# A macaron decoder layer: how the feed-forwards are multiplied, and how their sums reach the residual

## The chip, the core and the metric

The kernel runs on one core of a Trainium2 chip. Its engines are TensorE (matmuls; PE in the profile, its weight loads PEld), VectorE (DVE), ScalarE (ACT), GpSimd (POOL) and SyncE (SP, which here only issues DMAs). Each engine works through its own instruction queue in order, and semaphores make one wait for another. The metric is the device time of one execution in microseconds: the median of three runs is 2218.06 us (2217.84 to 2219.36).

## What is computed

One decoder layer over 256 tokens of width 2048, in float32: a feed-forward, a token mixer, a cross-attention, a second feed-forward and a final norm. The change touches the two feed-forwards:

```python
def rms_norm(x, g):
    xf = x.astype(jnp.float32)
    y = xf * lax.rsqrt(jnp.mean(xf * xf, axis=-1, keepdims=True) + NORM_EPS)
    return (y * g.astype(jnp.float32)).astype(x.dtype)

def swiglu(h, w_gate, w_up, w_down):
    return (jax.nn.silu(h @ w_gate) * (h @ w_up)) @ w_down

x = x + 0.5 * swiglu(rms_norm(x, ffn1_norm[l]), ffn1_w_gate[l], ffn1_w_up[l], ffn1_w_down[l])
...
x = x + 0.5 * swiglu(rms_norm(x, ffn2_norm[l]), ffn2_w_gate[l], ffn2_w_up[l], ffn2_w_down[l])
```

w_gate and w_up are 2048 x 5632, w_down is 5632 x 2048.

## The kernel before, in words

**A product in three matmuls.** Every float32 operand is split into two parts, `hi` (rounded, by ScalarE) and `lo` (what is left, by VectorE); a product is then hi*hi + hi*lo + lo*hi, three matmuls (`times`, L442 to L444). The stationary operand is 128 rows of x by 128 tokens, the moving one 128 rows by 512 columns of a weight. The sum of a product grows in a PSUM bank of 128 x 512; banks come from three rings, `acc` (3), `mm` (3) and `tr` (2, also used for transposes).

**Units, items, blocks.** A weight matrix is walked in column blocks of 512. A unit is two row groups of 128 x 512 (0.5 MB) of one block. An item is what the loop takes next (`next_item`, L401): one unit, or a pair of units of two matrices. A feed-forward has eleven column blocks j of gate and up, in groups of 4, 4 and 3, and behind each group the rows of w_down that belong to it, as two products: columns 0 and 512 together (first half), then 1024 and 1536 (second half).

**Seven products in place of eight.** From block 1 on, gate and up (and in w_down two column blocks) are multiplied together by `product_pair` (L502). For an ordinary pair q of rows it makes 2 token halves x 2 matrices x 2 row groups = 8 products, 24 matmuls. For the pairs listed in `SEVEN` (0, 2, 4) it makes seven products of sums and differences, 21 matmuls. These need sums of the weights (four VectorE steps, L394 to L397, split again by L373 and L374) and sums of x (`combinations`, L454, made once per feed-forward for x and once per group for the hidden values). `SEVEN_DOWN` does the same for w_down: (2, 4, 6) in the first half of a group of four, (2, 4) elsewhere (the second half of the last group of the second feed-forward is not paired). After the last of the seven-product pairs `middle` adds the banks p1, p5, p6, p7 into shared sums, and after the last pair `out` adds the other banks, p2, p4, p3, p5, as they end. In w_down each of these steps ends in x += 0.5 * bank (L603).

**Block 0** is not paired: first all eight units of gate (`product`, bank `acc`), then all eight of up (bank `mm`), while x_t, the transposed x, is still coming in by DMA in pieces (`chunks`) between the first weight loads. Features of x are made from x_t as it comes, and x itself is loaded later (`tokens`) for the mean square, whose root `norm.r` is needed only at the end of the block.

**What sets the order.** `next_item` issues the loads ahead on SyncE, in the order of the plan, and splits at most two units (one pair) ahead. There are three buffers of `hi` and of `lo`, one of each of the split weight sums (`thi`, `tlo`, a and b), and four of the 1 MB weight tiles; a load waits until its buffer is free. Between matmuls the loop ticks a set of generators (`Interleave`), which issue the transposes, the combinations of x and the loads of x a piece at a time. The program order is then rearranged once, ahead of the run, by a scheduler that goes by planned costs: it puts each engine's instructions in the order in which it expects their inputs, so that TensorE may take a later product ahead of one whose operand it expects late. On the chip these queues are fixed.

In the second feed-forward (`last`) the pairs with seven products are `SEVEN_2` = (0, 2, 3, 4); the weight sums of pair 3 are made earlier, in the mixer, and staged in DRAM at the items `STAGE_AT`.

## Time and profile before

| | |
|---|---|
| median of three runs | 2218.06 us (2217.84 to 2219.36) |
| the profiled execution | 2216.97 us |
| its span, first to last instruction | 2215.2 us |
| TensorE matmul busy | 2200.2 us (99%), 10520 matmuls |
| VectorE busy | 1829.0 us (83%) |
| ScalarE busy | 1250.0 us (56%) |
| DMA | 466.02 MB, mean 210 GB/s |

In the rows that follow, "out<-in" are the program's own names, then come the shapes, the count (x...), and, in a view by groups, the busy time and the mean duration of one, and behind a bar the idle time just before and what ended it. In a view in order of time a row begins with its start and its duration, and brackets at the end hold the idle time before it and its cause. In a view by stretch the busy time of each engine is followed by its count of instructions. L numbers are lines of the kernel before.

### The profile page before, as it was taken

How to read it: one execution, taken by the hardware profiler on the slowest of the kernel's cores; microseconds unless marked ns; L12 is line 12 of the kernel's file. 1: busy time of each engine (PE TensorE's matmuls, PEld its weight loads, DVE VectorE, ACT ScalarE, POOL GpSimd, SP SyncE). 2: the span in 40 equal slices, each digit the busy share in tenths (PEclk: the TensorE clock that was granted, in tenths of full speed). 3: DMA queues.
4: the chain of work that ended last, by engine and by line, in shares of the span. 5: the costliest groups of instructions: out<-in, count | busy, mean ns of one | idle time of the engine just before them, and what ended most of it. 6: DMA issues, size and time to landing. Idle time of an engine off the chain costs nothing.

```text
span 2215.2 us, 28140 instructions
## 1 busy us (share of the span) xinstructions
PE 2200.2 (99%) x10520; PEld 1817.0 (82%) x10520; DVE 1829.0 (83%) x2348; ACT 1250.0 (56%) x1621; POOL 107.0 (5%) x185
## 2 busy tenths in 40 slices
PE   9999999999999999999999999999999999999998
PEld 7888888888888877788888888888888888888886
DVE  7999988898989476977667666558999999999997
ACT  7555555555556477644544546556565565555654
POOL 0000000000000000000331130001000000000000
PEclk9999999999999999999999999999999999999999
DMA  8555555555556545676768687547665666665573
GB/s 306 199 207 198 194 200 201 198 199 194 200 194 204 178 130 165 197 237 210 223 224 287 209 273 270 183 164 280 220 221 190 212 227 211 214 208 208 200 244 135
DMA packets 231560, 466.02 MB, mean 210 GB/s; under 512 B 15520, under 2 KB 17920, under 8 KB 231424
## 3 DMA queue, kind: packets, MB, share of 16 engines
q1 hardware_dynamic: 222256, 438.08, 58.4%
q0 software_dynamic: 7648, 23.52, 3.5%
q10 hardware_dynamic: 1520, 2.63, 0.3%
q8 instruction: 82, 1.34, 0.3%
q14 instruction: 54, 0.44, 0.1%
HBM read 440.49 MB, written 23.59 MB: 209 GB/s over the span
## 4 chain that ended last, share of the span: by engine, by line
PE 94%; DVE 3%; DMA 1%; issue 1%; ACT 1%; SPq 0%; POOLq 0%; POOL 0%; DVEq 0%; ACTq 0%
PE acc L442 19%; PE acc L443 19%; PE acc L444 19%; PE mm L443 8%; PE mm L444 8%; PE mm L442 8%; PE tr L443 2%; PE tr L630 2%; PE tr L442 2%; PE tr L444 2%; PE mm L1425 1%; DVE lo L366 1%; DMA raw<-in_ffn_w_up_dram 1%; PE tr L1355 0%; ACT hi L365 0%
## 5 line engine op out<-in xcount | busy, mean ns | idle before, releaser
L365 ACT CAST hi<-raw 128x1024 fp32r<-128x1024 f32 (+1 forms) x768 | 755.1, 993 | 687.7 <-PE acc L444 485.9
L366 DVE TENSOR_TENSOR lo<-raw,hi 128x1024 fp32r<-128x1024 f32 (+1 forms) x768 | 878.8, 1147 | 291.8 <-ACT hi L365 289.3
L442 PE MATMUL acc<-hi,xhi 128*128 128x512 f32 (+1 forms) x1134 | 445.7, 394 | 2.0 <-DVE ga L1278 1.5
L443 PE MATMUL acc<-lo,xhi 128*128 128x512 f32 (+1 forms) x1134 | 439.9, 388 | 0.8 <-DVE lo L366 0.8
L444 PE MATMUL acc<-hi,xlo 128*128 128x512 f32 (+1 forms) x1134 | 439.7, 388 | 0.0
L442 PEld LDWEIGHTS acc<-hi,xhi 128*128 128x128 f32 x1134 | 213.2, 188 | 47.8 <-issue 3.1
L444 PEld LDWEIGHTS acc<-hi,xlo 128*128 128x128 f32 x1134 | 212.9, 188 | 43.5 <-issue 0.4
L443 PEld LDWEIGHTS acc<-lo,xhi 128*128 128x128 f32 x1134 | 213.4, 188 | 42.7 <-DVE lo L366 2.2
L373 ACT CAST thi<-raw 128x1024 fp32r<-128x1024 f32 x192 | 200.3, 1052 | 69.1 <-DVE raw L396 45.0
L374 DVE TENSOR_TENSOR tlo<-raw,thi 128x1024 fp32r<-128x1024 f32 x192 | 232.1, 1217 | 0.9 <-ACT thi L373 0.3
L442 PE MATMUL mm<-hi,xhi 128*128 128x512 f32 x402 | 156.6, 389 | 0.1
L443 PE MATMUL mm<-lo,xhi 128*128 128x512 f32 x402 | 156.5, 389 | 0.0
L444 PE MATMUL mm<-hi,xlo 128*128 128x512 f32 x402 | 156.4, 389 | 0.0
L444 PE MATMUL acc<-hi,hlo 128*128 128x512 f32 x372 | 145.4, 391 | 0.0
L443 PE MATMUL acc<-lo,hhi 128*128 128x512 f32 x372 | 145.3, 391 | 0.0
L442 PE MATMUL acc<-hi,hhi 128*128 128x512 f32 x372 | 145.0, 390 | 0.0
L442 PEld LDWEIGHTS mm<-hi,xhi 128*128 128x128 f32 x402 | 75.4, 188 | 16.2 <-ACT hi L365 0.5
L443 PEld LDWEIGHTS mm<-lo,xhi 128*128 128x128 f32 x402 | 75.5, 188 | 15.8
L444 PEld LDWEIGHTS mm<-hi,xlo 128*128 128x128 f32 x402 | 75.5, 188 | 15.7
L442 PEld LDWEIGHTS acc<-hi,hhi 128*128 128x128 f32 x372 | 69.9, 188 | 14.3
L443 PEld LDWEIGHTS acc<-lo,hhi 128*128 128x128 f32 x372 | 69.8, 188 | 14.3
L444 PEld LDWEIGHTS acc<-hi,hlo 128*128 128x128 f32 x372 | 69.9, 188 | 14.0
(443 smaller groups left out, 3526.6 us busy)
## 6 DMA issues: line engine op xcount, KB each, us to landing
raw<-in_ffn_w_down_dram SPq DMA_DIRECT2D x88, 1024.0 KB, 5.2
raw<-in_ffn_w_gate_dram SPq DMA_DIRECT2D x84, 1024.0 KB, 5.1
raw<-in_ffn_w_up_dram SPq DMA_DIRECT2D x78, 1024.0 KB, 6.0
raw<-in_w_in_dram SPq DMA_DIRECT2D x136, 512.0 KB, 3.8
...
```

Of the source, the lines that this page charges most:

```text
L365: at["hi"] = act.copy(hi[:, s], raw[:, s])
L366: at["lo"] = dve.tensor_tensor(lo[:, s], raw[:, s], f32(hi[:, s]), ALU.subtract)
L373: act.copy(hi[:], v[:])
L374: dve.tensor_tensor(lo[:], v[:], f32(hi[:]), ALU.subtract)
L442: pe.matmul(o, xh, hi, start=first, stop=False, **how)
L443: pe.matmul(o, xh, lo, start=False, stop=False, **how)
L444: pe.matmul(o, xl, hi, start=False, stop=last, **how)
L630: pe.transpose(b[:, o : o + P], tok[:, t, col : col + P], ident[:])
L1425: pe.matmul(vb[to, (o + k) * P : (o + k + 1) * P][:, r], lhs(k, e), v[:, k, r], start=v is u and k + e == 0, stop=True, **ek,)
```

## The change

- **Block 0 of the first feed-forward**: gate and up become one paired entry of eight items, multiplied by the new `plain_pair`: for every pair of row groups first gate (two `acc` banks), then up (two `mm` banks), 24 matmuls an item. The first loads on SyncE are put in that order: gate and up alternate, and the pieces of x_t follow their use. The first four units are split by halves. The loads of x and the squares are tied to other items (4 and 5 up to 7, of 8).
- **Seven more pairs with seven products** in the first feed-forward: blocks 3, 5, 7, 9, 10 use pairs (0, 2, 4, 6); blocks 4, 6, 8 use (2, 4, 6); blocks 1 and 2 keep (0, 2, 4). The second half of w_down uses (2, 4, 6) in the groups of four. Combinations of x are made for pair 6 too, from item 19 on. An early ordinary pair without a combination (pair 5, and pair 0 in blocks 4, 6, 8) adds its last product to a further bank, "q", as w_down did already, so `out` has one more addition.
- **w_down, both feed-forwards**: before the first matmul of a product pair, ScalarE writes twice x into the four banks p2, p4, p3 and q; the matmuls add to it, and what comes out is halved. `first` and `middle` then write into x itself. A pair has eight VectorE steps in place of twelve, and five ScalarE steps in place of one.
- Two constant tiles that nothing used ("shift", "pad") go; the staging is bound to items eight lower, since there are eight items fewer.

```diff
-                yield (wg, wu), 0, KD, (j * 512, j * 512), SEVEN_2 if last else SEVEN
+                seven = SEVEN_MORE if j in MORE else SEVEN_LATER if j in LATER_ON else SEVEN
+                seven = SEVEN_2 if last else seven
+                yield (wg, wu), 0, KD, (j * 512, j * 512), seven
...
+SEVEN_MORE, MORE = (0, 2, 4, 6), (3, 5, 7, 9, 10)
+SEVEN_LATER, LATER_ON = (2, 4, 6), (4, 6, 8)
 SEVEN_2, STAGED = (0, 2, 3, 4), (3,)
-STAGE_AT = [266 + 2 * n for n in range(10)]
+STAGE_AT = [258 + 2 * n for n in range(10)]
...
+            if j == 0 and not last:
+                yield (wg, wu), 0, KD, (0, 0), ()
...
-            yield (wd, wd), 4 * j0, 4 * nj, (1024, 1536), SEVEN_DOWN[1]
+            yield (wd, wd), 4 * j0, 4 * nj, (1024, 1536), SEVEN_DOWN[last or nj < 4]
...
-        for s in (slice(0, 1), slice(1, 2)) if u < AHEAD else (rows,):
+        for s in (slice(0, 1), slice(1, 2)) if u < 2 * AHEAD else (rows,):
...
+        for to, there in onto:
+            b[to] = rings[to]()
+            act.activation(b[to][:], there, AF.Copy, scale=2.0)
+            begun.add(to)
...
+    def plain_pair(sp, x: Act, norm, w):
+        pw, _, nk, _, seven = plan[at["product"]]
+        assert pw[0].tensor is w.tensor and not seven
+        at["product"] += 1
+        hb = sp.tile([P, 2, 512], F32, tag="hb", name="hb", bufs=2)
+        g2_, u2_ = [acc() for _ in range(2)], [mm() for _ in range(2)]
+        for k in range(0, nk, KU):
+            bg.until(lambda: all(k + i in x.done for i in range(KU)))
+            for wt, o in zip(next_item(), (g2_, u2_)):
+                for t in range(2):
+                    multiply(o[t][:], x, wt, k, t, nk)
+                    bg.tick()
+        bg.until(lambda: norm.r is not None)
+        for t in range(2):
+            act.activation(hb[:, t, :], g2_[t][:], AF.Silu, scale=norm.r[t])
+            dve.scalar_tensor_tensor(
+                hb[:, t, :], u2_[t][:], norm.r[t], hb[:, t, :], ALU.mult, ALU.mult
+            )
+        return hb
...
+                for z in (to, "q") if t and "q" in b else (to,):
+                    dve.tensor_tensor(v[:], b[z][:], v[:], ALU.add)
...
+    def down(h: Act, c, w, xs):
+        (x00, x01), (x10, x11) = xs
+        def half(x_, v, y):
+            dve.scalar_tensor_tensor(x_, v, 0.5, y, ALU.mult, ALU.add)
         def first(b):
-            act.copy(u3[:], b["p1"][:])
-            half(xs[0][0], b["p1"][:])
-            half(xs[1][1], b["q"][:])
+            act.activation(x00, b["p1"][:], AF.Copy, scale=0.5)
         def middle(b):
-            dve.tensor_tensor(u2[:], b["p6"][:], u3[:], ALU.add)
-            dve.tensor_tensor(u3[:], b["p7"][:], u2[:], ALU.add)
-            dve.tensor_tensor(u2[:], b["p5"][:], u2[:], ALU.add)
-            half(xs[1][0], u3[:])
-            half(xs[1][1], u3[:])
-            half(xs[0][1], u2[:])
+            half(x01, b["p6"][:], x00)
+            half(x10, b["p7"][:], x01)
+            half(x01, b["p5"][:], x01)
+            half(x11, b["q"][:], x10)
         def out(b, to):
-            half(xs[int(to in ("p4", "p5"))][int(to in ("p3", "p5"))], b[to][:])
-        product_pair(h, c, w, first, middle, out)
+            x_ = xs[int(to in ("p4", "p5"))][int(to in ("p3", "p5"))]
+            half(x_, b[to][:], x_)
+        product_pair(
+            h, c, w, first, middle, out, (("p2", x00), ("p4", x10), ("p3", x01), ("q", x11))
+        )
...
+            lambda q: (
+                at["item"] > begun + (18 if q > 4 and not last else 4)
+                and not (last and norm.r is None)
+            ),
+            less=(1,) if last else (1, 3),
...
+        load(2, [(slice(0, 2), nc.sync)])
         chunks(2, 2)
-        load_rest(0, 2, 1)
-        load_rest(0, 3, 1)
+        load_rest(0, 2)
+        load_rest(2, 2)
         chunks(4, 2)
-        load(2, [(slice(0, 2), nc.sync)])
+        load(4, [(slice(0, 2), nc.sync)])
+        load(6, [(slice(0, 2), nc.sync)])
         chunks(6, 2)
-        load_rest(2, 2)
+        load_rest(4, 2)
+        load_rest(6, 2)
         chunks(8, 4)
-        load(4)
         chunks(12, 4)
-        load(6)
         n1.begin(turned)
         def tokens(n):
-            while at["item"] < 7 + n:
+            while at["item"] < 4 + n // 2:
                 yield
             with tc.issue_after(at["hi"].ins):
                 act.dma_start(col(n), blk(W["x"], n))
-            while at["item"] < 10 + n:
+            while at["item"] < 5 + (n + 1) // 2:
...
```

61 lines of the change are left out of this document (26 added, 35 removed).

## Prediction

> **What bounds the kernel now.** I read the page first (busy shares, chain), then the busy time by stretch, then the waits of VectorE and ScalarE, then the order of time at the start and around a block of gate and up. The page:
>
> ```profile
> span 2215.2 us, 28140 instructions
> PE 2200.2 (99%) x10520; PEld 1817.0 (82%) x10520; DVE 1829.0 (83%) x2348; ACT 1250.0 (56%) x1621; POOL 107.0 (5%) x185
> PE 94%; DVE 3%; DMA 1%; issue 1%; ACT 1%; SPq 0%; POOLq 0%; POOL 0%; DVEq 0%; ACTq 0%
> raw<-in_ffn_w_gate_dram SPq DMA_DIRECT2D x84, 1024.0 KB, 5.1
> raw<-in_ffn_w_up_dram SPq DMA_DIRECT2D x78, 1024.0 KB, 6.0
> ```
>
> The chain is TensorE for 94%. The next view gives the first feed-forward as two stretches (busy time of each engine, then clock, DMA share, GB/s), two blocks inside it (j = 5 and 6), and five microseconds of the start:
>
> ```profile
> 4.92:52.08 47.16, 45.59 (x194) 36.02 (x193) 37.68 (x65) 35.09 (x60) 2.22 (x3) 1.00 0.94 343
> 52.08:710.10 658.02, 657.96 (x2949) 543.60 (x2949) 603.83 (x750) 367.24 (x417) 1.47 (x2) 1.00 0.57 198
> ...
> 306.20:348.60 42.40, 42.40 (x193) 35.20 (x192) 38.73 (x47) 24.49 (x28) 0.00 (x0) 1.00 0.58 199
> 348.60:390.90 42.30, 42.30 (x192) 35.14 (x191) 38.10 (x49) 23.34 (x26) 0.00 (x0) 1.00 0.57 199
> ...
> 20.00:25.00 5.00, 5.00 (x24) 4.10 (x23) 4.32 (x7) 2.95 (x5) 0.00 (x0) 1.00 1.05 386
> ```
>
> From 52.08 on TensorE is always busy, but VectorE is close behind: 603.8 of 658.0 us (92%), 54 us idle. The waits say what that idle time is:
>
> ```profile
> DVE lo L366 <- ACT hi L365: 39.0, 47, 1.8
> DVE raw L394 <- DMA raw<-in_ffn_w_up_dram: 4.8, 8, 0.9
> ...
> ACT hi L365 <- PE acc L444: 123.9, 94, 2.9
> ACT hi L365 <- PE mm L444: 72.7, 48, 2.1
> ```
>
> VectorE waits for ScalarE's `hi`, and ScalarE waits for TensorE to give back one of the three `hi` buffers. So VectorE idles because it has caught up, and those 39 us are its reserve.
>
> **Durations.** TensorE, in order of time (start, duration):
>
> ```profile
> 4.92 1.20 PE L442 MATMUL acc<-hi,xhi 128*128 128x512 f32 x2
> ...
> 7.49 0.50 PE L442 MATMUL acc<-hi,xhi 128*128 128x512 f32 x1 [0.52 <-ACT hi L669]
> ...
> 9.23 0.61 PE L442 MATMUL acc<-hi,xhi 128*128 128x512 f32 x2
> ...
> 44.18 0.39 PE L442 MATMUL mm<-hi,xhi 128*128 128x512 f32 x1
> ...
> 51.43 0.39 PE L444 MATMUL mm<-hi,xlo 128*128 128x512 f32 x1
> 52.08 0.73 PE L442 MATMUL tr<-thi,chi 128*128 128x512 f32 x2 [0.26 <-ACT thi L373]
> ```
>
> Between 44.18 and 51.43 lie 32 matmuls: 7.25 / 32 = 0.2266 us each, whatever their listed 0.39. VectorE overlaps in the same way; before and after block 6 begins at 348.6:
>
> ```profile
> 325.82 0.68 DVE L366 TENSOR_TENSOR lo<-raw,hi 128x512 fp32r<-128x512 f32 x1
> 327.92 1.23 DVE L366 TENSOR_TENSOR lo<-raw,hi 128x1024 fp32r<-128x1024 f32 x1 [1.42 <-ACT hi L365]
> ...
> 349.46 0.68 DVE L394 TENSOR_TENSOR raw<-raw,raw 128x512 f32<-128x512 f32 x1
> 350.06 0.74 DVE L593 SCALAR_TENSOR_TENSOR hb<-u,rs,hb 128x512 f32<-128x512 f32 x1
> 350.72 1.22 DVE L366 TENSOR_TENSOR lo<-raw,hi 128x1024 fp32r<-128x1024 f32 x1
> 351.86 0.68 DVE L395 TENSOR_TENSOR raw<-raw 128x512 f32<-128x512 f32 x1
> ...
> 354.80 1.22 DVE L374 TENSOR_TENSOR tlo<-raw,thi 128x1024 fp32r<-128x1024 f32 x1
> 355.94 1.81 DVE L366 TENSOR_TENSOR lo<-raw,hi 128x1024 fp32r<-128x1024 f32 x2
> ```
>
> Start to start: 0.60 for 128x512, 1.14 for 128x1024, 0.66 for the scaled one. An ordinary pair costs VectorE two `lo` = 2.3 us and TensorE 24 matmuls = 5.44 us. A pair with seven products costs VectorE four sums, three wide `lo` and a half one, 4 x 0.60 + 3 x 1.14 + 0.60 = 6.4 us, and TensorE 21 matmuls = 4.76 us.
>
> **The change, part by part.**
> Seven more pairs: five in blocks 3, 5, 7, 9, 10, two in the second halves of w_down. 7 x 3 = 21 matmuls leave TensorE: -4.76 us, on the path.
>
> VectorE in the first feed-forward: 7 x (6.4 - 2.3) = +28.7; one addition of the extra bank "q" in eight blocks, +4.8; one more combination of x (two 128x512 steps, four of 128x128), about +2; four steps fewer in each of six w_down pairs, -14.4. Net +21 us against 54 idle: 625 of about 653, 96%. On average it fits, so I cost it at nothing except where it bunches.
>
> It bunches where a block that ends with seven products at q = 6 is followed by one that begins with them: 4 to 5, 6 to 7, 8 to 9, 9 to 10. From the start of q = 6 to the first `lo` of the next block's q = 1 VectorE owes: `lo` of q = 7, 2.3; three sums, 1.8; two halves of the transposed block, 1.2; the next q = 0, 6.4; the ends of four banks with the extra one, 5 x 0.60 + 2 x 0.66 = 4.3 (and the last `lo`, 1.1): 17.1 us. TensorE needs 4.76 + 5.44 + 0.9 (transposes: 42.40 less 183 x 0.2266) + 4.76 + 0.2 = 16.1. So VectorE comes 1.0 us late if it works without a gap, and 2.4 us late if it idles 1.4 us at the start of q = 6, as it does at 327.92. Before, three ordinary pairs lay in between. What a lateness costs is shown once, in w_down, where the seven products' `tlo` came late:
>
> ```profile
> 191.66 1.22 DVE L374 TENSOR_TENSOR tlo<-raw,thi 128x1024 fp32r<-128x1024 f32 x1
> ...
> 192.57 0.39 PE L444 MATMUL mm<-hi,hlo 128*128 128x512 f32 x1
> 192.93 0.50 PE L443 MATMUL tr<-tlo,dhi 128*128 128x512 f32 x1
> ```
>
> `tlo` was done at 192.88, a microsecond after TensorE began the pair at 191.66; TensorE had taken other products forward and lost 192.93 - 192.57 - 0.23 = 0.13 us there. In the late q = 1, 8 of the first 12 matmuls need no `lo`, 1.8 us of cover. So a lateness of 1.0 costs next to nothing, one of 2.4 some 0.6 to 1.0 us. I take 0.5 for each of four places, +2.0, nearer to the row that shows cover; ends: 0 and 2.4 + 1.1 (one more wide `lo` late) = 3.5 each. Blocks 3, 7 and 10 run into w_down with the same queue plus one addition of 0.60; hidden as at 192.57, else 3 x 0.6 = 1.8.
>
> The start. 192 matmuls at 0.2266 are 43.5 us; from 4.92 to 52.08 are 47.16, so 3.7 us are lost. 1.6 of it lies before 9.23 (4.31 less 12 x 0.2266), waiting for the first weight rows, and stays. The rest is waiting for weights and features while DMA runs full (386 GB/s at 20 to 25 us), and 0.4 just before 52.08. Multiplied together, gate and up use each feature of x twice as long, so x_t and weights are wanted more slowly: by 4 + 4 pairs, not by 8 gate pairs. What ScalarE and VectorE wait for there:
>
> ```profile
> 6.82 0.62 ACT L669 CAST hi<-raw 128x512 fp32r<-128x512 f32 x1 [1.32 <-DMA raw<-in_ffn_w_gate_dram]
> ...
> 52.33 1.22 DVE L374 TENSOR_TENSOR tlo<-raw,thi 128x1024 fp32r<-128x1024 f32 x1
> ```
>
> Gate's second row is there at 6.8. In file order up's first rows (0.52 MB, 1.4 us at 386 GB/s) land near 8.2 and, behind 0.26 MB of x_t, gate's second pair (0.52 MB) near 10.2, against a need at 9.3 and 12.1 with 1.2 to 1.8 us of splitting. This fits, barely. After that the lead grows. The combinations of x begin at item 5 of 8 in place of 8 of 16, so at the same moment, and VectorE has 37.7 us of work in 47.2. I take 1.9 of the 2.1 us; ends -0.5 (a loss, if up's first rows come a `lo` late) and 2.6 (with the slips in block 1's first pairs). One more DMA is issued from SyncE; the queue is full anyway. The moved loads of x (4, on ScalarE's queue) and their squares end before the block does, as they do now. The banks of gate and up are held until 1/rms, as now.
>
> Twice x into four banks: 4 ScalarE steps for each of 11 w_down pairs. The nearest rows:
>
> ```profile
> L576 ACT COPY hb<-mm x20: 569/587/590, 75.3 to 2120.7; 128x512 f32<-128x512 f32 x20
> ...
> L365 ACT CAST hi<-raw 128x512 fp32r<-128x512 f32 x46 | 28.4, 620 | 24.3 <-PE acc L444 14.5 <-issue 6.2 <-ACT thi L373 3.2
> ```
>
> About 0.6 each, 2.4 per pair, 26 in all, on an engine busy 367 of 658; casts queued behind them have the idle 124 + 73 us above as cover. A bank that VectorE gives back late would hold the first matmul: 0.6 x 11 = 6.6 us if nothing hid it. But three of four banks are first touched 6 to 18 matmuls later, and p2 has 18 matmuls (4.1 us) of the pair before. 0, ends 0 and +6.6. VectorE's 20 steps fewer in the second feed-forward shorten no path there: 0, at best -0.5.
>
> The shift of the staging by eight items follows the eight items fewer: 0. The two unused constants that go move addresses only: 0; the trace shows no speed by address.
>
> Sum: -4.8 - 1.9 + 2.0 = -4.7 us. The profiled execution took 2216.97 (span 2215.2), 1.1 under the median of 2218.06; from the median I predict 2213.4. A measurement of this kernel tells about 0.2%, 4.4 us, from no change.
>
> **Rivals.**
> 1. VectorE's queue at the four changes of block decides (slower). For: 17.1 us owed against 16.1, and the 1.42 us idle at 327.92. Against: the cover at 192.57. With 3.5 at four places and 1.8 at w_down: -6.7 + 15.8, 2227. It makes the kernel slower by 0.2% from (6.7 + 4.4) / 4 = 2.8 us per place. Chance 0.12.
> 2. The gain is eaten: the start yields nothing, because VectorE, not DMA, brings block 1's first `tlo` (1.22 us long, while TensorE waited for `thi` at 52.08), and each place costs 1 us: -4.8 + 4 = -0.8, 2217.3. Chance 0.22.
> 3. Everything is covered: -4.8 - 2.1, 2211.2. For: TensorE reorders products around late operands. Chance 0.14.
> 4. VectorE is the bound of the first feed-forward throughout, so that its 21 us more come out in full, less the 1.9 of the start: 2237. Against: its 39 us of waiting for buffers that TensorE frees. Chance 0.02. The Trainium skill, "Perfetto Trace Analysis", Identifying the Most-Contended Engine, would say so: judge TensorE by its weight loads and VectorE by its occupancy, and the highest is the engine to relieve. Here that is 92% against 543.6 of 658 (83%); the trace does not agree, since matmuls follow each other at 0.2266 us without a gap.
>
> **Chances.** The forecast has 0.50, its own range 2212.0 to 2215.5 (0.2 to 0.8 us per place, start 1.2 to 2.1); about two thirds of it lie below 2213.6. Faster: 0.33 + 0.14 = 0.47; same: 0.17 + 0.22 = 0.39; slower: 0.12 + 0.02 = 0.14. The range reaches from 2210.5 (case 3 and the best of start) to 2220.0 (case 2 with 1.7 us per place), which leaves out cases 1 and 4 and little else.
>
> **What would show it.** Block 1 begins near 50.2, not 52.08, and matmuls before it still lose 1.6 us. The first feed-forward has 21 matmuls fewer and VectorE about 96% busy, its wait for `hi` well under 39 us. TensorE's gaps sit at q = 1 and 2 of blocks 5, 7, 9, 10: under 1 us each, or 3.5 under rival 1. The writes of 2x are never what a first matmul waits for. I am wrong if up's first rows starve TensorE before 15 us, if those gaps pass 2.8 us, or if the preload stands in the waits.

## The result and the profile after: slower by 0.5%

The changed kernel takes 2230.3 us (median of four runs, 2229.4 to 2231.2), the kernel before, run beside it on the same chip, 2218.3. The ratio is 1.0054 with an interval of 1.0041 to 1.0066. Forecast were 2213.4 us and a range that ended at 2220.0, so both the time and its sign were wrong.

The page of the changed kernel (span, busy shares, chain, loads; L numbers are from here on lines of the kernel that ran):

```profile
span 2229.3 us, 28212 instructions
PE 2204.1 (99%) x10499; PEld 1811.2 (81%) x10499; DVE 1836.4 (82%) x2362; ACT 1282.6 (58%) x1682; POOL 107.0 (5%) x185
PE 86%; DVE 7%; DMA 3%; ACT 1%; issue 1%; POOL 0%; SPq 0%; POOLq 0%; DVEq 0%; ACTq 0%
raw<-in_ffn_w_gate_dram SPq DMA_DIRECT2D x84, 1024.0 KB, 5.2
raw<-in_ffn_w_up_dram SPq DMA_DIRECT2D x76, 1024.0 KB, 6.3
```

TensorE does 21 matmuls fewer (10,499 for 10,520), as the plan says, and VectorE's share of the whole span has not grown (82.6% before, 82.4% now). On this page only the chain of work that ended last tells that something is wrong: TensorE holds 86% of it where it held 94%, and VectorE and DMA have taken most of the rest.

The busy time by stretch (length; busy time of TensorE, weight loads, VectorE, ScalarE, GpSimd; clock, DMA share, GB/s): block 0, the rest of the first feed-forward, and in it block 1, the first halves of w_down behind blocks 3 and 7, and block 7:

```profile
5.45:51.09 45.64, 45.32 (x192) 36.34 (x193) 36.17 (x61) 33.02 (x58) 1.96 (x3) 1.00 0.97 351
51.09:722.93 671.84, 661.90 (x2936) 538.36 (x2935) 626.53 (x792) 392.83 (x461) 2.18 (x3) 1.00 0.58 194
51.09:96.66 45.57, 43.99 (x192) 34.62 (x191) 41.17 (x54) 25.87 (x31) 0.00 (x0) 1.00 0.54 182
181.57:226.67 45.10, 43.62 (x193) 34.89 (x191) 42.87 (x60) 26.61 (x33) 0.00 (x0) 1.00 0.54 184
396.51:441.07 44.56, 42.96 (x189) 34.20 (x188) 43.51 (x58) 27.24 (x33) 0.00 (x0) 1.00 0.56 189
441.07:486.18 45.11, 43.62 (x192) 34.89 (x191) 42.87 (x60) 26.61 (x33) 0.00 (x0) 1.00 0.54 183
```

Before, TensorE's busy time of the second stretch was its length (657.96 of 658.02); now it is short of it by 9.9 us. That is not all of the loss: a matmul is listed with 0.39 us and followed by the next after 0.2266, so that a short wait does not show as idle time. The stretch is 13.8 us longer with 4.8 us less to do, which makes 18.6. VectorE's work has grown by 626.5 - 603.8 = 22.7 us, close to the 21 forecast, and 45 us of idle time are left to it. In the stages shown behind block 0 it is 90 to 98% busy.

The waits of three engines in that second stretch (engine, tile, line and what it waited for: total us, times, longest). In the changed kernel L369 and L370 make `hi` and `lo`, L398 is the first of the sums of weights, L617 empties the banks p2 and p4, L622 the banks p3, p5 and q:

```profile
DVE lo L370 <- ACT hi L369: 17.2, 27, 1.9
DVE raw L398 <- DMA raw<-in_ffn_w_up_dram: 15.2, 10, 3.2
DVE raw L398 <- DMA raw<-in_ffn_w_down_dram: 6.8, 4, 2.4
...
ACT hi L369 <- PE acc L448: 149.4, 89, 4.7
...
PE acc L446 <- ACT hi L369: 2.1, 3, 0.7
PE acc L446 <- DVE hb L617: 1.8, 3, 0.9
PE mm L446 <- ACT hi L369: 1.3, 3, 0.4
PE mm L447 <- DVE lo L370: 1.1, 3, 0.4
PE tr L446 <- ACT thi L377: 1.1, 1, 1.1
PE acc L447 <- DVE lo L370: 0.9, 1, 0.9
PE tr L659 <- DVE u L609: 0.8, 1, 0.8
```

The same view of the kernel before has one line for TensorE in all of this stretch:

```profile
PE tr L442 <- ACT thi L373: 0.3, 1, 0.3
```

So TensorE now waits at many places, about a microsecond or less each: for split weights, for banks not yet emptied (L617), for a bank that transposes go into (L609). And VectorE's idle time has changed its kind: 22 us of it are spent waiting for weights to land, for 5 before. That is no mark of loss by itself: in two runs further down it waits as long for weights (27.0 us in e7, 24.3 in e14), and their blocks lose 0.7 us and nothing. What counts is where it waits.

**Where the time lies.** I counted TensorE's 128x512 matmuls in the order in which they began (192 for block 0, 24 for an ordinary pair, 21 for one with seven products) and so cut the first feed-forward into its stages. What a stage takes beyond its count x 0.2266 us is its loss. The table gives matmuls and losses as differences to the kernel before, in us, for the changed kernel and for all runs below; "rest" is what comes after the first feed-forward. Each line adds up to the difference of its profiled span to the 2215.2 of before.

| run | seven pairs | matmuls | start, block 0 | block 1 | blocks 2-10 | w_down first halves (3) | second halves (3) | rest | span |
|---|---|---|---|---|---|---|---|---|---|
| changed kernel | 51 | -4.8 | -1.0 | +2.6 | +7.9 | +7.3 | +0.8 | +1.3 | +14.1 |
| e1 preload only | 44 | 0 | +1.0 | +0.1 | +0.1 | 0.0 | +1.0 | -0.6 | +1.5 |
| e2 sevens only | 51 | -4.8 | +0.7 | 0.0 | +8.1 | +5.6 | +0.4 | +2.7 | +12.6 |
| e3 block 0 only | 44 | 0 | -0.6 | +2.6 | +0.2 | 0.0 | 0.0 | -0.4 | +1.8 |
| e4 early extra bank | 51 | -4.8 | -0.2 | +2.6 | +8.8 | +3.1 | +0.9 | -0.1 | +10.2 |
| e6 less VectorE work | 51 | -4.8 | -0.8 | 0.0 | +6.3 | +0.7 | +2.4 | +0.6 | +4.5 |
| e7 later pairs | 46 | -1.4 | -0.8 | +2.6 | +0.7 | +7.3 | +0.7 | -0.6 | +8.5 |
| e8 x early | 44 | 0 | +6.2 | +1.4 | +0.1 | 0.0 | +0.1 | +0.7 | +8.4 |
| e9 four only at the ends | 49 | -3.4 | -0.8 | +2.6 | +3.0 | +3.1 | +2.1 | +0.2 | +6.9 |
| e10 half tiles | 51 | -4.8 | -1.3 | +2.6 | +8.0 | +7.3 | +1.0 | +0.7 | +13.6 |
| e11 no extra bank | 46 | -1.4 | -1.0 | -0.2 | -0.1 | +3.1 | +2.3 | -1.3 | +1.5 |
| e12 e11, half tiles | 46 | -1.4 | -1.2 | +0.5 | +1.7 | +3.0 | +0.9 | -0.7 | +3.0 |
| e13 early bank, half tiles | 51 | -4.8 | -1.3 | +2.6 | +10.9 | +3.1 | +0.9 | +1.8 | +13.3 |
| e14 e11, free end | 43 | +0.7 | -0.5 | -0.2 | 0.0 | 0.0 | +1.0 | -0.8 | 0.0 |
| e15 rest of change | 45 | -0.7 | -1.4 | -0.5 | +2.2 | 0.0 | +1.2 | +0.3 | +1.0 |
| e16 q = 1, 3, 5 | 46 | -1.4 | -1.0 | +1.4 | +0.4 | +0.3 | +2.0 | -0.2 | +1.4 |
| e17 e16, block 1 later | 45 | -0.7 | -0.7 | 0.0 | +0.3 | +0.2 | +1.5 | -1.2 | -0.6 |
| e18 e14 again | 43 | +0.7 | -1.7 | -0.2 | -0.1 | 0.0 | +1.0 | 0.0 | -0.3 |

The rest and block 0 differ between profiled executions whose program is the same there: block 0 of e14 and e18, one kernel, by 1.2, and the rest by 2.7 between e2 and the kernel before, with the same instructions in the same order. So nothing is read from them below that. Of the last second half, 0.7 to 1.0 us in every run with the preload is no waiting: TensorE does 24 transposes of x there in place of 16. The loss lies in three places: block 1, the changes of block, and the first halves of w_down.

**The three places in the trace of the changed kernel.** The first is the change from one block to the next, here from block 6 to block 7, which begins at 396.51. VectorE in order of time (start, duration, in brackets the idle time ahead and what ended it), and below it SyncE's loads:

```profile
373.19 0.68 DVE L370 TENSOR_TENSOR lo<-raw,hi 128x512 fp32r<-128x512 f32 x1
376.05 0.69 DVE L398 TENSOR_TENSOR raw<-raw,raw 128x512 f32<-128x512 f32 x1 [2.17 <-DMA raw<-in_ffn_w_up_dram]
...
379.72 1.22 DVE L370 TENSOR_TENSOR lo<-raw,hi 128x1024 fp32r<-128x1024 f32 x1
...
386.44 0.69 DVE L398 TENSOR_TENSOR raw<-raw,raw 128x512 f32<-128x512 f32 x1 [1.50 <-DMA raw<-in_ffn_w_up_dram]
...
396.93 0.68 DVE L617 TENSOR_TENSOR hb<-acc,hb 128x512 f32<-128x512 f32 x1
```

```profile
378.50 0.37 SPq L320 DMA_DIRECT2D raw<-in_ffn_w_gate_dram  x1
380.97 0.37 SPq L320 DMA_DIRECT2D raw<-in_ffn_w_up_dram  x1
```

Up's weights for the next seven pair are asked for at 380.97, the moment at which the `lo` begun at 379.72 is done with the buffer. 5.4 us later they are there. Until then VectorE stands, although behind it lies the densest work of the block. Then the banks come free late (L617 at 396.93), and TensorE, at 397.67, has waited for one. It had also stood at 391.87, in the last pair of block 6, for a bank that transposes go into:

```profile
391.87 0.66 PE L659 MATMUL tr<-ident,hb 128*128 128x128 f32 x4 [0.76 <-DVE u L609]
```

So what block 6 loses belongs to this change too. The change from block 4 to block 5 shows the same in a milder form: VectorE idles 1.46 us for up's weights at 301.69, it empties the first bank at 312.18, behind the splits for the new block, and TensorE stands for it:

```profile
312.92 0.50 PE L446 MATMUL acc<-hi,xhi 128*128 128x512 f32 x1 [0.87 <-DVE hb L617]
```

The second place is the end of block 3. VectorE and ScalarE in order of time:

```profile
184.04 0.68 DVE L622 TENSOR_TENSOR u<-mm,u 128x512 f32<-128x512 f32 x1
...
186.38 0.68 DVE L622 TENSOR_TENSOR u<-acc,u 128x512 f32<-128x512 f32 x1
...
190.67 1.22 DVE L370 TENSOR_TENSOR lo<-raw,hi 128x1024 fp32r<-128x1024 f32 x1 [1.81 <-ACT hi L369]
```

```profile
187.10 0.60 ACT L517 ACTIVATE acc<-x 128x512 f32<-128x512 f32 x1 [1.24 <-DVE u L622]
189.59 1.05 ACT L369 CAST hi<-raw 128x1024 fp32r<-128x1024 f32 x1 [1.89 <-PE acc L448]
```

The extra bank is emptied last, at 186.38, five microseconds into w_down. Until then ScalarE's write of 2x into it waits (187.10) with the casts behind it. TensorE takes other products first and so gives the `hi` buffers back later (189.59), and VectorE idles 1.81 us in the middle of its work. It never gets level again: TensorE's gaps come at 195 to 199 us.

The third place is the start of block 1, whose first pair now has seven products and needs `thi` at once. ScalarE, then TensorE:

```profile
48.58 0.62 ACT L369 CAST hi<-raw 128x512 fp32r<-128x512 f32 x1
49.22 1.28 ACT L590 ACT_TABLE_LOAD   x1
50.51 1.27 ACT L590 ACTIVATE hb<-acc,rs 128x512 f32<-128x512 f32 x2
51.67 1.04 ACT L377 CAST thi<-raw 128x1024 fp32r<-128x1024 f32 x1
```

```profile
51.32 0.39 PE L447 MATMUL mm<-lo,xhi 128*128 128x512 f32 x1
52.76 0.73 PE L446 MATMUL tr<-thi,chi 128*128 128x512 f32 x2 [1.05 <-ACT thi L377]
```

Loading the table and block 0's two Silu stand in front of the cast of `thi`, which ends at 52.71. TensorE stands 1.44 - 0.23 = 1.2 us, and more behind it. The sums that this cast reads had been ready at 49.76 (L400 on VectorE).

### The profile page after: what moved, and what is told of

Its sections match the earlier page's. It is cut to its first block, busy times and chain, and to the rows that moved or that the text cites. A ratio compares the mean times of both kernels' runs of the same rounds, so it can differ in the third digit from the quotient of the medians.

```text
span 2229.3 us, 28212 instructions
## 1 busy us (share of the span) xinstructions
PE 2204.1 (99%) x10499; PEld 1811.2 (81%) x10499; DVE 1836.4 (82%) x2362; ACT 1282.6 (58%) x1682; POOL 107.0 (5%) x185
## 4 chain that ended last, share of the span: by engine, by line
PE 86%; DVE 7%; DMA 3%; ACT 1%; issue 1%; POOL 0%; SPq 0%; POOLq 0%; DVEq 0%; ACTq 0%
PE acc L446 18%; PE acc L447 18%; PE acc L448 18%; PE mm L447 7%; PE mm L448 7%; PE mm L446 7%; DVE lo L370 2%; DMA raw<-in_ffn_w_up_dram 2%; PE tr L447 2%; PE tr L448 2%; PE tr L659 2%; PE tr L446 2%; PE mm L1458 1%; ACT hi L369 1%; DVE tlo L378 1%
## 5 line engine op out<-in xcount | busy, mean ns | idle before, releaser
L369 ACT CAST hi<-raw 128x1024 fp32r<-128x1024 f32 (+1 forms) x770 | 752.4, 987 | 670.5 <-PE acc L448 505.8
L370 DVE TENSOR_TENSOR lo<-raw,hi 128x1024 fp32r<-128x1024 f32 (+1 forms) x770 | 875.0, 1141 | 279.3 <-ACT hi L369 276.4
L377 ACT CAST thi<-raw 128x1024 fp32r<-128x1024 f32 x206 | 214.9, 1051 | 75.3 <-DVE raw L400 52.6
L378 DVE TENSOR_TENSOR tlo<-raw,thi 128x1024 fp32r<-128x1024 f32 x206 | 249.6, 1219 | 2.3 <-ACT thi L377 1.6
L448 PEld LDWEIGHTS acc<-hi,xlo 128*128 128x128 f32 x1141 | 214.2, 188 | 43.7 <-issue 0.4
L447 PE MATMUL mm<-lo,xhi 128*128 128x512 f32 x365 | 142.3, 390 | 0.0
L448 PE MATMUL mm<-hi,xlo 128*128 128x512 f32 x365 | 142.1, 389 | 0.0
L446 PE MATMUL mm<-hi,xhi 128*128 128x512 f32 x365 | 140.9, 390 | 0.1
L398 DVE TENSOR_TENSOR raw<-raw,raw 128x512 f32<-128x512 f32 x93 | 63.9, 687 | 34.3 <-DMA raw<-in_ffn_w_up_dram 23.8
L448 PEld LDWEIGHTS acc<-hi,hlo 128*128 128x128 f32 x370 | 69.5, 188 | 14.1
L446 PEld LDWEIGHTS mm<-hi,xhi 128*128 128x128 f32 x365 | 68.4, 188 | 15.2 <-ACT hi L369 0.5
L447 PEld LDWEIGHTS mm<-lo,xhi 128*128 128x128 f32 x365 | 68.5, 188 | 14.8 <-DVE lo L370 0.4
```

Of the source, the lines that this page charges most:

```text
L369: at["hi"] = act.copy(hi[:, s], raw[:, s])
L370: at["lo"] = dve.tensor_tensor(lo[:, s], raw[:, s], f32(hi[:, s]), ALU.subtract)
L377: act.copy(hi[:], v[:])
L378: dve.tensor_tensor(lo[:], v[:], f32(hi[:]), ALU.subtract)
L398: dve.tensor_tensor(t[1][:, 0], ru[:, 0], rg[:, 0], ALU.subtract)
L446: pe.matmul(o, xh, hi, start=first, stop=False, **how)
```

## The experiments

**Parts of the change alone.** e1 is the kernel before with 2x written into the banks of w_down, and nothing else of the change:

```diff
+        for to, there in onto:
+            b[to] = rings[to]()
+            act.activation(b[to][:], there, AF.Copy, scale=2.0)
+            begun.add(to)
```

> The kernel before with twice x written into the banks of w_down, and nothing else of the change. Theory (shared bank): the preload hurts only where the block ahead of w_down also holds a third acc bank, its extra bank q; here no block of the first feed-forward has one, so the first halves of w_down keep their 42.7 us each and the time is that of before, 2217 to 2219. Rival (the preload itself): each of eleven w_down pairs waits some 0.6 us for ScalarE, 2224 to 2225.

Measured: 2218.4 us in a single run, 0.6 over the 2217.8 of before on that chip. The three first halves of w_down take what they took (0.0 in the table). By itself the preload costs nothing that can be told from the scatter.

e2 is the changed kernel without the preload and with block 0 as before, so that the seven pairs more are left:

```diff
-            if j == 0 and not last:
-                yield (wg, wu), 0, KD, (0, 0), ()
-            elif j == 0:
+            if j == 0:
...
-        product_pair(
-            h, c, w, first, middle, out, (("p2", x00), ("p4", x10), ("p3", x01), ("q", x11))
-        )
+        product_pair(h, c, w, first, middle, out)
```

> The kernel before with the seven more pairs alone: w_down as before, block 0 as before. Theory (shared bank): w_down's product q still needs the acc bank that the block's q gives back late, so the first halves of w_down lose 1 to 2.4 us each even without the preload; blocks 5, 6, 7 and 10 lose about 1 us each beside their 0.68 of gain; 2220 to 2226. Rival (the preload blocks ScalarE, in order): the first halves stay at 42.7 us, 2217 to 2219. Rival (VectorE is short of time): without the steps that the preload saves it is worse than the changed kernel, over 2230.

Measured: 2229.5 us, 11.8 over before and over the 2220 to 2226 that I had given. The seven pairs carry nearly all of the loss: 8.1 us in the blocks and 5.6 in the first halves of w_down. With the preload the latter are 7.3, so the preload does cost 0.6 per first half once the extra bank comes back late.

e3 is the kernel before with block 0 multiplied together:

```diff
-            if j == 0:
+            if j == 0 and not last:
+                yield (wg, wu), 0, KD, (0, 0), ()
+            elif j == 0:
```

> The kernel before with block 0 of gate and up multiplied together alone. Theory (Silu in the way): block 1's first products come 1.4 us late because the table load and Silu of block 0 stand before their cast on ScalarE, as in the changed kernel: block 0 is 1.5 us shorter, block 1 2.6 us longer, 2218.5 to 2219.5. Rival (VectorE has more to do in the changed kernel's block 1): block 1 keeps its 43 us, 2216 to 2217.

Measured: 2218.7 us, 0.9 over before. Block 0 is 0.9 us shorter, block 1 2.6 longer. This part loses by itself, and in the same place as in the whole change.

**The first halves of w_down.** e4 is the changed kernel with the extra bank added as the third of the five, behind p2 and p4 and ahead of p3 and p5:

```diff
+                if t and "q" in b:
+                    dve.tensor_tensor(u3[:], b["q"][:], u3[:], ALU.add)
             else:
                 v = u3 if t else u2
-                for z in (to, "q") if t and "q" in b else (to,):
-                    dve.tensor_tensor(v[:], b[z][:], v[:], ALU.add)
+                dve.tensor_tensor(v[:], b[to][:], v[:], ALU.add)
```

> The changed kernel, with one step moved: the block's extra bank q is added to the shared sum right behind p4's step, not behind p5 at the very end. Theory (shared bank): q's bank comes free some 2 to 3 us sooner, w_down's preload and its q product no longer stand, and the first halves of w_down fall from 45.1 (34.9 in the last group) to at most 43.5 (33): 2223 to 2226. Rival (VectorE is short of time): as much work in another order, first halves within 0.5 us of 45.1, 2229 to 2231.

Measured: 2227.1 us, with the first halves at 43.7 and 33.5, just over what I had given. They lose 3.1 us in all for 7.3: one VectorE instruction moved ahead of the steps of two other banks gives 1.4 us each. Of the 2.4 us of each half a rest of 1.0 stayed, which e14 explains.

**VectorE's work.** e6 is the changed kernel with less for VectorE to do in each seven pair of the first feed-forward. It leaves out two of the four weight sums, and makes the second pair of split parts from gate's weights themselves:

```diff
+            if g < ends[0]:
+                dve.tensor_tensor(t[0][:, 0], ru[:, 1], ru[:, 0], ALU.subtract)
+                dve.tensor_tensor(t[0][:, 1], ru[:, 1], rg[:, 0], ALU.subtract)
+                a_ = two_parts(t[0], "a")
+                parts[i] = split_unit(g), split_unit(u, slice(1, 2)), (a_, two_parts(rg, "b"))
+                return
```

> The changed kernel with two of the four weight sums of every seven-product pair of the first feed-forward left out, and the second split made from gate itself: the output is not the reference's. TensorE, ScalarE and DMA have the same work, VectorE 1.2 us less per such pair. Theory (VectorE's queue at the changes of block): blocks 5, 6, 7, 10 and the first halves of w_down come back to within 0.3 us of the stretch without waits (41.7, 42.4, 41.7, 41.7; 42.4 and 32.2): 2217 to 2220. Rival (the third acc bank is missing, whoever is late): they lose as much as in the changed kernel, 2228 or more.

Measured: 2221.5 us, 8.8 under the changed kernel and between the two forecasts. Block 1 and the first halves are cured (0.0 and +0.7), the blocks are not (+6.3). In the first halves the extra bank is emptied last here as well, so what a late bank costs depends on how late VectorE is. In block 1 the fixed order has changed: ScalarE casts `thi` at 49.62, ahead of the table load at 50.68, and TensorE waits for nothing. The stretch behind block 0, and in it VectorE's waits:

```profile
51.30:713.97 662.67, 657.63 (x2936) 538.75 (x2935) 568.53 (x691) 390.88 (x460) 2.18 (x3) 1.00 0.59 196
```

```profile
DVE lo L370 <- ACT hi L369: 39.6, 39, 2.5
DVE raw L399 <- DMA raw<-in_ffn_w_up_dram: 34.9, 19, 4.0
```

VectorE has 568.5 us of work here, 35 us less than in the kernel before, and still TensorE loses 6 us between the blocks. So the amount of VectorE's work alone does not decide there. Its wait for up's weights has grown to 34.9 us, and that is not spread evenly: 4.7 of the 6.3 us are lost at the change from block 6 to block 7, where VectorE idles longest, between the two seven pairs:

```profile
382.13 0.69 DVE L399 TENSOR_TENSOR raw<-raw 128x512 f32<-128x512 f32 x1 [3.98 <-DMA raw<-in_ffn_w_up_dram]
```

At the other changes it idles 2.65, 2.65 and 1.87 us for weights, and they lose 1.0, 0.7 and 0.1. Much of the work taken away from VectorE has become waiting in the same place.

**Distance between seven pairs.** e7 is the changed kernel with seven products at q = 2, 4, 6 in all blocks from 3 to 10, so that none of these blocks begins with a seven pair:

```diff
-SEVEN_MORE, MORE = (0, 2, 4, 6), (3, 5, 7, 9, 10)
-SEVEN_LATER, LATER_ON = (2, 4, 6), (4, 6, 8)
+SEVEN_MORE, MORE = (0, 2, 4, 6), ()
+SEVEN_LATER, LATER_ON = (2, 4, 6), (3, 4, 5, 6, 7, 8, 9, 10)
```

> The changed kernel with pairs (2, 4, 6) in all of blocks 3 to 10: no block has four, each has the extra bank q, and every change of block has a plain pair 0 behind a pair 6 with seven products. Theory (bunching at the change of block): blocks 4 to 10 run at 41.5 to 42.5 us; two pairs in w_down are all that is gained, the first halves of w_down keep 44 to 45: 2223 to 2226. Rival (the extra bank in each block): blocks 4 to 10 still lose a microsecond each, 2228 to 2232. Rival (only block 1 and the start cost): 2218.

Measured: 2225.5 us.

```profile
51.25:719.23 667.98, 661.89 (x2951) 542.58 (x2950) 608.29 (x762) 384.73 (x451) 2.18 (x3) 1.00 0.59 195
```

The blocks lose 0.7 us where the change loses 7.9, with 608.3 us of VectorE work, 40 more than in e6 and 4.5 more than before. Blocks 3 to 10 all have the extra bank here, so it is not what costs there. What costs in the blocks is a seven pair at the end of one right ahead of a seven pair at the start of the next. This run has five seven pairs fewer than the change; that their number is not the cause is shown by e9, where blocks 7 and 10 have four each and lose nothing. The first halves of w_down keep their 7.3: there the late bank and the pair at q = 6 are still in place.

e9 puts four seven pairs only into blocks 3, 7 and 10, which run into w_down, leaves q = 0, 2, 4 to the others and has the early bank of e4:

```diff
-SEVEN_MORE, MORE = (0, 2, 4, 6), (3, 5, 7, 9, 10)
-SEVEN_LATER, LATER_ON = (2, 4, 6), (4, 6, 8)
+SEVEN_MORE, MORE = (0, 2, 4, 6), (3, 7, 10)
+SEVEN_LATER, LATER_ON = (2, 4, 6), ()
```

> The changed kernel with q added early, four seven-product pairs only in blocks 3, 7 and 10, which run into w_down, and (0, 2, 4) in the others. Theory (bunching): the only seven-after-seven changes left are from w_down into blocks 4 and 8, which lose 0.5 to 2 us each; blocks 5, 6 and 9 are at 42.4 as before, 7 and 10 at 41.8; the first halves of w_down stay at 43.7: 2219 to 2223. Rival (VectorE's total): blocks 7 and 10 lose as before, over 44 us each, 2224 or more.

Measured: 2223.8 us, a little over what I had given. Blocks 5, 6, 7, 9 and 10 lose nothing now. Blocks 4 and 8 lose 1.2 us each, and these are the two behind a second half of w_down that has q = 6 as a seven pair: the same neighbourhood at another boundary, at a price of the same kind.

**Block 0's features.** e8 is e3 with the loads of x, whose squares give 1/rms, two items earlier:

```diff
-            while at["item"] < 4 + n // 2:
+            while at["item"] < 2 + n // 2:
...
-            while at["item"] < 5 + (n + 1) // 2:
+            while at["item"] < 4 + (n + 1) // 2:
```

> Block 0 multiplied together alone, with x loaded from item 2 on in place of 4, and the squares from item 4. Theory (Silu in the way): 1/rms is there 4 to 5 us sooner, Silu and its table load leave block 1's first cast free, block 1 falls from 45.5 to about 43: 2215.5 to 2217. Rival (VectorE and the combinations are late there): block 1 stays within 0.5 us of 45.5, 2218 to 2219.

Measured: 2225.3 us. Block 1 gets 1.2 us back (44.3 us, not the 43 of my theory), and block 0 loses 7.0 (53.31 us for 46.29): DMA is full there, and x takes the place of weights. TensorE stands once for long, for the `hi` of weights that landed late:

```profile
34.36 0.79 PE L446 MATMUL mm<-hi,xhi 128*128 128x512 f32 x1 [4.17 <-ACT hi L369]
```

That is not the whole loss: from 32.72 to 39.54 us the granted clock was 0.50, and matmuls followed each other at 0.427 us in place of 0.2266; for the 12 matmuls in it that is some 2.4 us more. An earlier 1/rms is not to be had in this way.

**Weight tiles of half the size.** e10 is the changed kernel with tiles of 0.5 MB in eight buffers, in the first feed-forward (w_down's too), loaded in the order of use:

```diff
+        if wide and u < ends[0]:
+            for i in range(m if pieces else 1):
+                raws[u + i] = at["pool"].tile([P, KU, n], F32, tag="raw2", name="raw2", bufs=8)
...
+        ahead = range(u, u + (2 * LOADED if at["pool"] is not None else LOADED))
+        if u < ends[0]:
+            ahead = sorted(ahead, key=lambda v: (v // 4, v % 2, v))
+        for v in ahead:
```

> The changed kernel with one thing else: gate's and up's weights are loaded in tiles of 0.5 MB into eight buffers in place of tiles of 1 MB into four, and the loads follow the order of use (gate q, up q, gate q + 1, up q + 1). A buffer is given back after half as many splits, so a load does not wait for the last split of its other half. Theory that the returned buffer decides (a late split gives its weight buffer back late, the next load lands late, VectorE idles where it can least afford it): VectorE's wait for weights between 265 and 645 us, 17.8 us in the changed kernel, falls under 6; blocks 5, 6, 7 and 10, which lose 0.9 to 2.2 us each over blocks that lose nothing, lose under 0.5; the first halves of w_down stay at 45.1; about 2224 us. Theory that VectorE's own work decides: the wait for weights falls, its wait for hi grows by as much, the blocks keep their loss, 2228 to 2231.

Measured: 2230.5 us, no gain. VectorE's waits in the stretch behind block 0:

```profile
DVE lo L383 <- ACT hi L382: 25.1, 30, 2.5
DVE raw L411 <- DMA raw<-in_ffn_w_up_dram: 13.6, 11, 2.9
```

My forecast for the returned buffer failed, and that for VectorE's own work came true. With w_down's 1.5 the wait for weights went down from 22.0 to 15.1 us, and the wait for `hi` went up by 8. Between 265 and 645 us the wait for weights was 13.3 and not under 6, so the run does not show what weights in time would do. The loss of blocks 5, 6, 7 and 10 did shrink from 6.5 to 2.1 us, but blocks 4 and 8, which had lost nearly nothing, took 3.4 and 1.6. These are the same changes of block, 4 to 5 and 8 to 9: TensorE now stands in the last pair of the old block (308.76 us, with block 5 beginning at 312.60) in place of the first pair of the new one. VectorE idles there between the two seven pairs:

```profile
305.14 0.69 DVE L411 TENSOR_TENSOR raw<-raw,raw 128x512 f32<-128x512 f32 x1 [2.94 <-DMA raw<-in_ffn_w_up_dram]
```

At 562.60, in the change from 8 to 9, it idles 1.84 us. From 6 to 7 and from 9 to 10 it does not wait for weights here, and what is lost there shrank from 3.8 and 1.1 us to 0.9 and 0.2. So within one kernel the loss went with the late weights. Why they are late at two changes and not at the others I have not settled.

e13 has both, the early bank and the half-size tiles (the two diffs above together):

> The changed kernel with both cures: the extra bank is added right behind the third of the four banks, and weight tiles are of 0.5 MB in eight buffers. If the two losses are separate, the gains add: first halves of w_down at 43.7 (as with the early bank alone) and blocks 5, 6, 7, 10 under 0.5 us of loss each, about 2220 us. If both are VectorE's lack of time, the early bank's gain stays and the blocks keep their loss: 2226 us.

Measured: 2230.2 us, outside both forecasts. The early bank gives the first halves the same 4.2 us as in e4, the blocks lose 3 us more than in e10. Part of that is the clock: it was 0.50 from 307.84 to 311.25 us, behind a wait of 2 us, and block 4 loses 4.4 where block 8, at full clock, loses 3.4. The cures do not add.

**No extra bank, and no seven pair behind another.** e11 is the changed kernel with q = 2, 4, 6 in all blocks from 1 to 10 and combinations of half the kind for q = 0, 1, 3, 5 (in what was expected of this run and the next ones, "products" are matmuls):

```diff
-SEVEN_MORE, MORE = (0, 2, 4, 6), (3, 5, 7, 9, 10)
-SEVEN_LATER, LATER_ON = (2, 4, 6), (4, 6, 8)
+SEVEN_MORE, MORE = (0, 2, 4, 6), ()
+SEVEN_LATER, LATER_ON = (2, 4, 6), range(1, 11)
...
-            sp, norm.x, SEVEN_2 if last else SEVEN_MORE, "c",
+            sp, norm.x, SEVEN_2 if last else SEVEN_LATER, "c",
...
-                at["item"] > begun + (18 if q > 4 and not last else 4)
+                at["item"] > begun + 4
...
-            less=(1,) if last else (1, 3),
+            less=(1,) if last else (0, 1, 3, 5),
```

> The changed kernel with seven products at q = 2, 4, 6 in every block of gate and up from 1 to 10 (15 products more than the change has) and with the combinations of x for q = 0, 1, 3 and 5 made so that a block needs no extra bank; the combinations start at item 5. So nothing of a block is given back behind its four banks. Block 0, w_down and its preload are as in the change. Theory of the two bunches (a block's q = 6 into the next q = 0, and the extra bank before w_down): blocks 4 to 10 at 42.4 us as with the same pairs before, first halves of w_down back from 45.1 to 42.7 to 43.3 (the 0.4 to 0.6 above 42.7 being the preload), second halves at 41.5, block 1 between 42.4 and 43.4: 2214 to 2218 us. Rival, that the preload itself makes the first halves of w_down late: they stay above 44, 2220 or more.

Measured: 2218.9 us, ratio to before 1.0003 (0.9993 to 1.0012), over my range. Blocks and block 1 lose nothing, and the first halves lose 1.0 each, as in e4, though there is no extra bank: that 1.0 has another cause.

e12 is e11 with the tiles of e10:

> The run before (seven products at q = 2, 4, 6 in all blocks, no extra bank in a block) with weight tiles of 0.5 MB in eight buffers. Theory of the returned buffer: what is left of VectorE's wait for weights goes, 0 to 1.5 us less than the run before, most of it in block 1 and behind w_down. Rival, that these blocks have cover enough: within 0.5 us of it. A loss of over 1 us would say that twice as many transfers of half the size cost something themselves.

Measured: 2220.7 us, ratio 1.0012 (1.0002 to 1.0022). Half-size tiles cost 1.7 us in the blocks here. That was the outcome named last. Between 265 and 645 us VectorE waits 7.8 us for weights, for 21.3 in e11, and nothing is gained by it: in the blocks of e11, where the seven pairs are apart, late weights had cost nothing.

e14 is e11 with the pair q = 6 of blocks 3, 7 and 10 made ordinary:

```diff
-SEVEN_MORE, MORE = (0, 2, 4, 6), ()
+SEVEN_MORE, MORE = (2, 4), (3, 7, 10)
```

> The run without extra banks (seven products at q = 2, 4, 6 in all blocks), with the pair q = 6 of blocks 3, 7 and 10 alone made ordinary again: 9 products more, 2.0 us of TensorE. Theory that the seven pair at q = 6 is what makes the first halves of w_down late: they go from 43.7 to 42.7 each, blocks 3, 7 and 10 take 0.68 more than 42.4, others as they were; in all 1 us less than the run it comes from, about 2217.5. Rival, that VectorE's other work or the preload of 2x makes them late: they stay at 43.5 or more, and the whole is 1.5 to 2 us slower than the run it comes from, about 2220.5.

Measured: 2216.9 us.

```profile
51.55:710.92 659.37, 659.37 (x2960) 545.20 (x2959) 595.21 (x741) 381.32 (x446) 2.35 (x4) 1.00 0.59 197
```

The first halves are at 42.7 us as before, and TensorE is busy all through the stretch: w_down wants two ordinary pairs at the end of the block ahead of it, where a block is content with one if it begins with two. The 2.4 us of each first half are 1.0 for the seven pair at q = 6 and 1.4 for the extra bank, 0.6 of which the preload adds. Both hold for VectorE as busy as it is in the changed kernel: in e6 they came to 0.2 together.

e15 keeps what is left of the change, w_down's seven pairs included: q = 0, 2, 4 in the blocks as before, block 1 with q = 2, 4 and the extra bank, added early, for its q = 0:

```diff
-SEVEN_MORE, MORE = (0, 2, 4, 6), (3, 5, 7, 9, 10)
-SEVEN_LATER, LATER_ON = (2, 4, 6), (4, 6, 8)
+SEVEN_MORE, MORE = (2, 4), (1,)
+SEVEN_LATER, LATER_ON = (2, 4, 6), ()
...
-            sp, norm.x, SEVEN_2 if last else SEVEN_MORE, "c",
+            sp, norm.x, SEVEN_2 if last else SEVEN, "c",
```

> What is left of the change when its crowded pairs are taken out: block 0 multiplied together, 2x in the banks of w_down, seven products at q = 6 more in the second halves of w_down of the first two groups; gate and up as before with q = 0, 2, 4, but block 1 with q = 2, 4 alone and the extra bank for its q = 0, added early. Theory that a seven pair at q = 0 right behind block 0 makes block 1 late: block 1 at 43.0 to 43.4 (183 + 3 products at 0.2266 and 0.9 of transposes are 43.1), block 0 at 46.2, second halves of w_down 41.5, all else as before: 42.95 - 43.1 + 1.0 + 1.36 = 1.2 to 2.0 us faster than before, 2216.4 to 2217.2. Rival, that the extra bank makes block 1 late: block 1 at 45 or more, about 2219.

Measured: 2217.8 us, ratio 0.9997 (0.9988 to 1.0006). Block 1 takes 43.1 us and loses nothing but its transposes, with the extra bank in it: it is the seven pair at q = 0 that made it late. Blocks 4 and 8 lose 1.1 and 0.8 behind the second halves with q = 6, as in e9. I had left this out, and so the time is over the 2216.4 to 2217.2 that I had given.

e16 has q = 1, 3, 5 in all blocks from 1 on, so that two ordinary pairs end every block and at least two lie between seven pairs across any boundary:

```diff
-SEVEN_LATER, LATER_ON = (2, 4, 6), range(1, 11)
+SEVEN_LATER, LATER_ON = (1, 3, 5), range(1, 11)
...
-            less=(1,) if last else (0, 1, 3, 5),
+            less=(1,) if last else (0, 2, 4),
```

> As the run without extra banks, with seven products at q = 1, 3, 5 in every block from 1 to 10 and combinations of half the kind at q = 0, 2, 4; w_down as in the change: 6 products fewer than before. Theory that only the distance between seven pairs across a boundary counts: blocks 2, 3, 5, 6, 7, 9, 10 at 42.4, 4 and 8 at 41.5, first halves of w_down 42.7, second halves 41.5, block 0 near 46.2; block 1 at 42.4 to 43.5; in all 1.5 to 2.5 us faster than before. Rival, that VectorE's amount of work decides, here as much as in the run without extra banks: some blocks or first halves lose 1 us as there, 2218 to 2220.

Measured: 2218.0 us, ratio 0.9999 (0.9990 to 1.0008). Blocks 2 to 10 lose 0.4 us together and the first halves 0.3, with 46 seven pairs for the 44 of before: the theory of distance holds there. Blocks 4 and 8 are at 41.5 us. Only block 1 loses, 1.4, and with that the gain of 1.5 to 2.5 us that I had expected is gone.

e17 gives block 1 of e16 q = 3, 5 alone, with the early bank:

```diff
-SEVEN_MORE, MORE = (0, 2, 4, 6), ()
+SEVEN_MORE, MORE = (3, 5), (1,)
```

> The run above with block 1 at q = 3, 5 alone, 3 products (0.68 us) more. If the combinations of x are late for q = 1 of block 1, block 1 loses less than there and the whole is up to 1 us faster than it; if they are in time, it is 0.7 us slower.

Measured: 2216.6 us, ratio 0.9994 (0.9985 to 1.0003). Block 1's loss goes, with three products more.

e18 is the kernel of e14 again, in more runs:

> The kernel of e14 once more, timed against the kernel before: sum of its stages against before -0.4 (block 0) - 0.2 (block 1) - 1.36 (second halves) + 1.9 (three pairs made ordinary) + 1 (end of the third group) = +0.9 by the stages up to the end of the first feed-forward, yet 1.7 under before in its one time: 0.9990 to 1.0004 of before.

Measured: 2217.0 us, ratio 0.9995 (0.9986 to 1.0004). e17 and e18 are the fastest that I found, 13 us under the changed kernel, and neither is shown to be faster than the kernel before.

## Why the prediction was wrong, step by step

Forecast were -4.7 us: -4.8 of TensorE, -1.9 at the start, +2.0 at the changes of block. The profile gives +14.1. The signs of the first two terms were right; the third was a quarter of what came, and block 1 and the first halves of w_down, both at nothing, took 2.6 and 7.3. The step that failed is the cover for a late VectorE. It was read at 192.57, where only an operand was late; here TensorE wants first the banks that VectorE gives back late.

- **21 matmuls, -4.8.** Right: 10,499 for 10,520, and a second half of w_down with its new pair, where nothing else stands in the way, went from 42.16 to 41.48 us.
- **VectorE's work, +21 us, at nothing on average.** The size was right (22.7), and that the total alone does not decide is shown by e6 against e7: 568.5 us of work with 6.3 us lost in the blocks, 608.3 with 0.7.
- **The 39 us of waiting for `hi` as a reserve.** Wrong as it was used. Time in which VectorE waits in ordinary pairs cannot be kept for a bunch, because buffers let it work only so far ahead: up's load at 380.97 us was issued as the last `lo` that read its buffer ended. In the changed kernel the wait for `hi` fell to 17.2 us, and 22 us of waiting for weights came in its place.
- **The change of block, +2.0.** The places and the mechanism were right, the price was not. Measured over the losses of before, with the end of a block counted to the change that follows it: 4 to 5 1.8, 6 to 7 3.8, 8 to 9 0.4, 9 to 10 1.1; block 2, not on the list, 0.7; in all 7.9. The allowance of 1.4 us of idle time for the worst was met at three of the four changes (1.46, 1.50 and 1.33 us, for weights), but 6 to 7 had 2.17 us more at 376.05, in the pair ahead. What failed is the cover. It counted only products that need no late `lo`, as seen at 192.57, and held a lateness of 2.4 us for 0.6 to 1.0 of loss. Here TensorE's first stand is for something else: the bank of the old block that VectorE empties behind the splits for the new one (L617), at 312.92, 397.67 and 612.70 us, and at 391.87 a bank for transposes (L609). In e6 the work owed falls by 2 x 1.2 us to 14.7 against 16.1; with 3.98 us of idle time inside it the change from 6 to 7 is dearer than in the changed kernel, 4.7.
- **Blocks 3, 7 and 10 into w_down, 0, or 1.8 if not hidden.** The largest miss: 7.3. I counted the extra bank as an addition of 0.60 us on VectorE and not as a bank that TensorE and ScalarE want next. It is emptied last and costs 1.4 per half (e4). The seven pair at q = 6 costs 1.0 (e14) where it saves 3 x 0.2266 = 0.7. The cover that I named, seen at 192.57, belonged to a state in which VectorE was not late already.
- **The start, -1.9.** Block 0 with its start gave -1.0 (-1.5 by itself), near enough given its scatter. The slips in block 1 that I hoped to save became +2.6. I had asked whether the combinations of x and the weights would come in time, and not what stands in ScalarE's queue ahead of the first `thi`. Before, the table load and two Silu ended in time, 2.0 us ahead of block 1. Of the moved squares I had asked only that they end before the block does. They do, at 47.96 us, but 3.1 ahead of block 1, where they had ended at 45.66, 6.4 ahead of it. So 1/rms and the Silu behind it come later (the second Silu ends at 51.78 for 50.06 before), while block 1 begins a microsecond sooner. e15 shows that only the seven pair at q = 0 suffers by it, and e6 that it does not suffer with its cast ahead of the table load.
- **The preload at 0, ends 0 and +6.6.** Right alone (e1). In the whole change it adds 0.6 to each of three first halves, because a late bank holds its write and the write holds the casts behind it.
- **Rivals.** Rival 1 had the right sign and most of the places. It gave 2227 with 3.5 us at each of four places, which was too much for three of them, and 0.6 at w_down, which was far too little. Its limit of 2.8 us per place was passed in one place only; slower came from w_down and block 1. That its time lies near the measured one is partly luck, as these two misses are of opposite sign. Rival 4, VectorE as the bound by its amount, gave a time not far off for a wrong reason: e6 and e7 exclude it. The Trainium skill, "Perfetto Trace Analysis", Identifying the Most-Contended Engine, would call VectorE the engine to relieve by its 93% of this stretch. Relieving VectorE by 58 us (e6) did give 8.8 us, in block 1 and w_down, but left 6.3 us of loss in the blocks; with 40 us more work than that, and the seven pairs apart, the blocks lost 0.7 (e7). The Trainium skill, "Perfetto Trace Analysis", Optimization Strategy, holds that a repeated gap can mean too little room for the next tile, and names buffer count and tile size. VectorE's waits for weights look like such a gap. With tiles of half the size in twice as many buffers they shrank from 22.0 to 15.1 us and the kernel took 2230.5 us (e10), so that this was not the remedy here.

What stays open: how the price of a change of block divides between VectorE's work and its waiting for weights. Where VectorE does not wait for weights between two adjacent seven pairs, a change cost 1.1 (9 to 10 in the changed kernel), 0.9 and 0.2 us (e10). Where it does, the price ranges from 0.1 to 4.7, and the changes from 4 to 5 and from 8 to 9 in the changed kernel, with the same pairs and nearly the same wait (1.46 and 1.33 us), cost 1.8 and 0.4. Why up's weights are late at some changes and not at others is open as well.
